# Streaming pooling trunk: operands of three products stored as split pairs by the first input phase and loaded as they are by the second

## Chip, cores and metric

One Trainium2 chip, one core of it. The metric is device time in microseconds, the median of the runs of one kernel. Engines: PE multiplies matrices (PEld is its weight load), DVE is VectorE, ACT ScalarE, POOL GpSimd; SP only issues transfers. Each engine works through its own instructions in order.

## What is computed

The depth is one layer, so only the pooling mixer runs, between two RMS norms. The sequence has 4096 frames of 1024 channels, everything in float32.

```
normed = rms_norm(x, norm_w)
u, gate = split(normed @ in_w, 2)              # in_w: 1024 x 2048
pooled  = trailing means of u (windows 2, 4, 8, 16 by channel group) - u
mixed   = pooled @ group_w + group_b           # per group, 256 x 256
y       = mixed * scale * silu(gate)
out     = rms_norm(x + y @ out_w, final_w)
```

## The kernel before

**Matrix products.** The large products are done in Winograd's form of Strassen's scheme: seven products (P1 to P7) of half-sized blocks in place of eight, with sums formed ahead. PE takes float32r operands, so a float32 operand is split into a high and a low part, and a product is made of high x high, high x low and low x high: three passes. The split is two instructions, an ACT copy that rounds (`copy(dst[:, 0], src)`) and a DVE subtraction that gives the rest (`sub(dst[:, 1], src, dst[:, 0])`), both on 128x1024 elements, in `split` (lines 203 to 206). Nearly all instructions are recorded under line 79, that of the wrapper `InOrder`, so the profile's groups are told apart by their tiles.

**Phases.** The group maps are first folded into the input weights (line 466 on PE). Then come three phases, listed step by step at lines 1450 to 1452: `("a", b, i)`, the first input phase, over four blocks `b` of 1024 frames and the seven products `i` in the order P1, P2, P7, P6, P5, P4, P3; `("b", b, i)`, the second input phase, over the same blocks with the other half of the input weights; and `("o", b, i)`, the output phase, over eight blocks of 512 frames. A plain product is 48 matmuls of 128x512 (line 814, in `mm3`).  In the second phase P7 of blocks 1 to 3 is itself done by seven smaller products (`split_seven`, `product_seven`, line 760). The first phase computes the operands of the seven products from x (loaded transposed, normalised and summed in `form_in`), splits them for its own products, and stores the unsplit float32 operand in DRAM (`sd`, 512 KB a half); the second loads it again and splits it again.

**Operand tiles.** The split operand of a half (`h` = 0, 1) is an `op` tile of 128 x 2048 float32r, 1024 KB: high part, then low part. There are four, taken in turn by `next_op` (line 561), so that a plain product uses two and the product after next uses the same two again. In a plain product PE reads the first half's tile for the first half of its time and the second half's for the rest; P1 goes by banks and reads both to the end. The seven-part P7 uses all four; two are filled for P6 while it runs, and `third` (line 701) sets the order anew, so that P5 gets the tile of parts P5 and P3 and the tile of parts P2 and P4.

**Other tiles.** Loads and results live in 11 `st` and 8 `vt` tiles, handed out and taken back by `take` and `give` (lines 178 to 189); a slot that is given back may be written again when its last reader is done, a DMA among them.

**What sets the order.** The loop at line 1903 goes through the steps. At each it calls `load` three steps ahead (`load_in`, line 602), `split_step` for the next step (`split_in`, line 645), `form` two steps ahead, then `run` (the product and the eviction of its banks). The program is then ordered engine by engine: the order of these calls is the priority, and an instruction that is ready may be placed before one that is not; `issue_after` keeps a pair in order. In the first phase `split_halves` (line 573) issues the stores `sd` on POOL's queue, whose instructions there also are the stores and loads of the reciprocal norms (`rd`). SP's queue carries the loads of x, of `sd` and of weights, and the stores of the pooled result `yd` and of transformed output weights (`wod`, `pair`). In block 2 of the first phase a weight sum, T3, is formed on DVE from loads of `wvd` (`load_t3`, `save_t3`, lines 340 and 345). The split weights of P5, P4 and P3 for the output phase are stored as pairs (`pairs_d`) and loaded on POOL's queue straight into weight tiles (`load_w`, line 402).

Of the kernel before, what the change touches and what calls it, by code (L numbers as in the profile page):

```python
# [10 lines left out]
F32 = mybir.dt.float32  # L11
# [4 lines left out]
P = 128  # L16
D = 1024
S = 4096
H = 512
TB = 1024  # L20
NB = S // TB
# [10 lines left out]
P1, P2, P3, P4, P5, P6, P7 = range(1, 8)  # L32
# [54 lines left out]
def kernel(  # L87
# [37 lines left out]
    vector, scalar, gpsimd, sync = (  # L125
        InOrder(tc, e) for e in (nc.vector, nc.scalar, nc.gpsimd, nc.sync)
    )
# [5 lines left out]
    dram = ctx.enter_context(tc.tile_pool(name="dram", bufs=1, space=bass.MemoryType.DRAM))  # L133
# [44 lines left out]
    def take(pattern="p (a b) -> p a b", pool=None, **sizes):  # L178
        sizes = sizes or {"a": 2}
        if pool is None:  # L180
            spare = len(vt.free) > keep[0] or not st.free
            pool = vt if spare and vt.age() < st.age() else st
        return pool.take(lambda t: t[:, 0:D].rearrange(pattern, **sizes))
# [4 lines left out]
    def give(ap):  # L188
        next(p for p in (st, vt, early, early5) if id(ap) in p.used).give(ap)

    def add(dst, a, b):
        vector.tensor_tensor(out=dst, in0=a, in1=b, op=ALU.add)

    def sub(dst, a, b):
        return vector.tensor_tensor(out=dst, in0=a, in1=b, op=ALU.subtract)
# [7 lines left out]
    def split(dst, src):  # L203

        latest_copy[0] = copy(dst[:, 0], src).ins
        latest_split[0] = sub(dst[:, 1], src, dst[:, 0].bitcast(F32)).ins
# [18 lines left out]
        for i in (P5, P4, P3)  # L225
    }
    sd = [
        {
            i: [dram.tile([P, 2, H], F32, name=f"sd{b}_{i}_{h}") for h in range(2)]
            for i in range(P1, P7 + 1)  # L230
            if (b, i) != (0, P6)
        }
        for b in range(NB)
    ]
# [180 lines left out]
    def woven(ap):  # L415

        return ap.rearrange("p (s a) -> p a s", s=2)
# [143 lines left out]
    def next_op(pattern, **sizes):  # L561
        t = ops.pop(0)
        ops.append(t)
        return t.rearrange(pattern, **sizes)
# [3 lines left out]
    def split_half(u):  # L568
        t = next_op("p (s a b) -> p s a b", s=2, a=2)
        split(t, u)  # L570
        return t

    def split_halves(us, saved=None):
        ts = []
        for h, u in enumerate(us):
            t = split_half(u)
            if saved is not None:
                first_saves.append(gpsimd.dma_start(out=saved[h], in_=u).ins)
            ts.append(t)
        return ts  # L580

    def load_x(b, half, kh, between=None):
        us = []
        for h in range(2):
            if h and between:
                between()
            u = take()
            k = 4 * kh + 2 * h
            sync.dma_start(out=u, in_=xt[2 * b + 1 - half, :, k : k + 2, :])
            us.append(u)  # L590
        return us

    def load_saved(b, i):
        us = []
        for h in range(2):
            u = take()
            sync.dma_start(out=u, in_=sd[b][i][h])
            us.append(u)
        return us
# [2 lines left out]

    def load_in(q, b, i):
        s = xs[b]
        if q and (b or i not in (P6, P4)):
            s[operand[i]] = load_saved(b, i)
        elif q:
            if i == P6:
                s["22"] = load_saved(b, P4)
        elif i in (P1, P2, P7, P6):  # L610
            key, *place = {
                P1: ("11", 0, 0), P2: ("12", 0, 1), P7: ("21", 1, 0), P6: ("22", 1, 1)
            }[i]
            s[key] = load_x(b, *place)
# [26 lines left out]
    def inner_in(q, b, i):  # L641

        return q == 1 and b > 0 and i == P7

    def split_in(q, b, i):
        s = xs[b]
        if inner_in(q, b, i):
            return split_seven(s)
        key = operand[i]
        later = q == 0 and b == 0 and i in (P1, P2)  # L650
        t = split_halves(s[key], None if q or later else sd[b].get(i))
        if later:
            stores.extend(zip(sd[0][i], s[key]))
        if i == P6 and q == 0 and b:
            form_s4(b)
        if q and (b or i != P7) or i not in (P1, P2, P7, P6):
            for u in s.pop(key):
                give(u)
        return t
# [5 lines left out]
    def split_seven(s):  # L665

        us = s["21"]
        a11, a21, a12, a22 = (
            us[h].rearrange("p k (s j a) -> p k s j a", s=2, j=2)[:, :, :, j]
            for h in range(2) for j in range(2)  # L670
        )
        front, back = (take("p (n k s a) -> p n k s a", n=2, k=2, s=2) for _ in range(2))
        sub(back[:, 0], a11, a21)
        sub(back[:, 1], a22, back[:, 0])
        add(front[:, 0], back[:, 1], a11)
        seven["mixed"] = sub(front[:, 1], a12, back[:, 1]).ins
        pattern = "p (s n k b a) -> p s n k b a"
        t = {}

        def sums(u, names):  # L680
            op = next_op(pattern, s=2, n=2, k=2, b=2)
            split(op.rearrange("p s n k b a -> p s (n k b a)"),
                  u.rearrange("p n k s a -> p (n k s a)"))
            give(u)
            for n, name in enumerate(names):
                t[name] = [[op[:, v, n, k].rearrange("p s a -> p a s") for k in range(2)]
                           for v in range(2)]

        def plain_op(h, names):
            op = split_half(us[h])  # L690
            for name, j in names.items():
                t[name] = [[woven(op[:, v, k])[:, j * P : (j + 1) * P] for k in range(2)]
                           for v in range(2)]

        sums(front, (P5, P3))
        plain_op(0, {P1: 0})

        def second():
            sums(back, (P7, P6))

        def third():
            plain_op(1, {P2: 0, P4: 1})
            for u in s.pop("21"):
                give(u)
            ops[:] = [ops[n] for n in (1, 2, 0, 3)]

        seven.update(second=second, third=third)
        return t
# [94 lines left out]
    def form_s4(b):  # L803
        for u, s2 in zip(xs[b]["12"], xs[b]["2"]):
            sub(u, u, s2)
# [652 lines left out]
    def load(n):  # L1458
        kind, b, i = step(n)
        if kind == "o":  # L1460
            load_o(b, i)
        elif kind:
            load_in(kind == "b", b, i)
# [13 lines left out]
    def split_step(n):  # L1477
        kind, b, i = step(n)
        if kind == "o":
            split_up[n] = split_o(b, i)  # L1480
        elif kind:
            with tc.issue_after(evicted[0]) if i == P6 else nullcontext():
                split_up[n] = split_in(kind == "b", b, i)
# [419 lines left out]
    for n in range(2, len(steps)):  # L1903
        kind, b, i = steps[n]
# [78 lines left out]
        if kind in ("a", "b"):  # L1983
# [11 lines left out]
            if kind == "b" and b == NB - 1 and i == P3:  # L1995
                f = take("p (a b) -> p a b", a=2)
                sync.dma_start(
                    out=f.rearrange("p a b -> p (a b)"), in_=final_w.partition_broadcast(P)
# [54 lines left out]
```

## Time and profile before

| | |
|---|---|
| median of 3 runs | 907.79 us (907.16 to 908.06) |
| span of the profiled execution | 905.6 us |
| time around the span, from that median | 2.2 us |
| busy PE, DVE, ACT, POOL | 99%, 81%, 57%, 17% of the span |
| moved by DMA | 209.60 MB, mean 231 GB/s |
| mean granted clock of PE | 0.999 |

The profile is of one execution; its own time apart from the span isn't listed, so the median stands for it. A group row reads: line, engine, operation, tile written <- tiles read, shape, count, then busy time in us, mean of one in ns, the engine's idle time just before, and what ended most of it. A row of the stages view reads: stretch, its length, busy time of each engine with its count, granted clock, share of the DMA engines' time, GB/s. A row of the timeline reads: start, duration, engine, line, operation, and in brackets the idle time before it and what ended it. "To landing" is the time from a DMA's issue to its last byte.

### The profile page before, as it was taken

What the parts mean: (1) busy time and instruction counts of PE and PEld (TensorE: products, weight loads), DVE (VectorE), ACT (ScalarE), POOL (GpSimd) and SP (SyncE); (2) the same over time, 40 slices, a digit from 0 to 9 for tenths busy, and PEclk for the clock granted to TensorE, in tenths of its full rate; (3) what the DMA queues carried; (4) which work ended last, traced back from release to release, by engine and by line L of the source; (5) the groups of instructions that cost most, each with busy time, mean ns of one, the idle gap of its engine ahead of it and who ended that gap; (6) DMA issues with size and microseconds to landing.
All of it is one profiled execution on the core that took longest, in us unless ns stands there. A gap on an engine that the chain in (4) does not pass through costs nothing.

```text
span 905.6 us, 12443 instructions
## 1 busy us (share of the span) xinstructions
PE 895.4 (99%) x4554; PEld 792.2 (87%) x4554; DVE 737.0 (81%) x910; ACT 519.2 (57%) x848; POOL 152.2 (17%) x250
## 2 busy tenths in 40 slices
PE   9999999999999999999999999999999999999996
PEld 7888888888888888889889888988889899998995
DVE  3899896984996996995485499698898788888798
ACT  7869547446445467446345654744557466565464
POOL 0030110110111000010100011021233343342330
PEclk9999999999999999999999999999999999999999
DMA  9989778678769475854245386699573855945953
GB/s 342 401 316 322 260 279 320 215 296 284 269 251 369 171 260 203 313 195 170 90 140 185 140 302 232 233 330 306 152 213 81 221 171 150 238 149 131 266 176 116
DMA packets 78620, 209.60 MB, mean 231 GB/s; under 512 B 7392, under 2 KB 25184, under 8 KB 77792
## 3 DMA queue, kind: packets, MB, share of 16 engines
q1 hardware_dynamic: 57872, 143.77, 45.7%
q0 software_dynamic: 19968, 63.98, 22.7%
q10 hardware_dynamic: 720, 1.06, 0.3%
q8 instruction: 35, 0.57, 0.3%
q14 instruction: 25, 0.20, 0.1%
HBM read 133.28 MB, written 75.51 MB: 231 GB/s over the span
## 4 chain that ended last, share of the span: by engine, by line
PE 88%; DVE 5%; DMA 3%; ACT 2%; issue 2%; POOL 0%; DVEq 0%; ACTq 0%; POOLq 0%; SPq 0%
PE bank L814 76%; PE bank L956 5%; PE bank L760 3%; PE bank L466 3%; DVE vt L79 2%; DVE op L79 2%; DVE st L79 1%; DMA vt<-yd 1%; DMA st<-wvd 1%; ACT vt L79 1%; DMA early<-in_group_w 0%; ACT st L79 0%; ACT op L79 0%; DMA out<-vt 0%; DVE columns L79 0%
## 5 line engine op out<-in xcount | busy, mean ns | idle before, releaser
L814 PE MATMUL bank<-op,w 128*128 128x512 f32 x2544 | 551.2, 379 | 1.5 <-ACT st L79 1.0
L814 PEld LDWEIGHTS bank<-op,w 128*128 128x128 f32 x2544 | 480.2, 189 | 70.9 <-ACT st L79 1.8
L814 PE MATMUL bank<-w,op 128*128 128x512 f32 (+1 forms) x1044 | 230.5, 377 | 0.0
L814 PEld LDWEIGHTS bank<-w,op 128*128 128x128 f32 x1044 | 192.3, 189 | 25.0
L79 DVE TENSOR_TENSOR op<-st,op 128x1024 fp32r<-128x1024 f32 x119 | 144.9, 1223 | 55.7 <-ACT op L79 55.4
L79 ACT ACTIVATE op<-st 128x1024 fp32r<-128x1024 f32 x119 | 124.8, 1052 | 81.6 <-PE bank L814 32.3
L79 ACT ACTIVATE op<-vt 128x1024 fp32r<-128x1024 f32 x66 | 69.4, 1053 | 70.0 <-DVE vt L79 41.7
L79 DVE TENSOR_TENSOR op<-vt,op 128x1024 fp32r<-128x1024 f32 x66 | 79.8, 1222 | 22.2 <-ACT op L79 22.1
L79 ACT ACTIVATE vt<-bank 128x512 f32<-128x512 f32 (+1 forms) x124 | 68.7, 577 | 46.0 <-PE bank L814 38.3
L79 DVE TENSOR_TENSOR st<-st,st 128x1024 f32<-128x1024 f32 (+2 forms) x49 | 54.8, 1134 | 30.4 <-ACT st L79 16.7
L79 ACT ACTIVATE bank<-bank 128x512 f32<-128x512 f32 (+1 forms) x84 | 41.1, 489 | 51.4 <-PE bank L814 38.6
L79 POOL COPY vt<-tails 128x32 f32<-128x32 f32 x14 | 17.5, 1257 | 271.7 <-DVE inner L79 106.8
L79 DVE TENSOR_TENSOR vt<-bank,vt 128x512 f32<-128x512 f32 (+1 forms) x92 | 52.9, 603 | 6.2 <-PE bank L956 4.6
L79 ACT ACTIVATE st<-bank 128x512 f32<-128x512 f32 (+1 forms) x60 | 34.2, 586 | 35.6 <-PE bank L814 25.0
L79 ACT ACTIVATE st<-st 128x1024 f32<-128x1024 f32 (+1 forms) x37 | 38.9, 1056 | 21.7 <-DVE st L79 19.7
L79 DVE TENSOR_TENSOR st<-bank,st 128x512 f32<-128x512 f32 (+1 forms) x70 | 42.6, 627 | 4.7 <-PE bank L956 2.5
L79 POOL DMA_DIRECT2D sd<-st x45 | 24.0, 533 | 125.7 <-DVE st L79 77.7
L956 PEld LDWEIGHTS bank<-w,op 128*128 128x128 f32 x312 | 40.4, 191 | 1.7
L956 PE MATMUL bank<-w,op 128*128 128x256 f32 x312 | 41.1, 275 | 0.0
L79 DVE TENSOR_TENSOR st<-st,vt 128x1024 f32<-128x1024 f32 (+1 forms) x33 | 38.5, 1187 | 2.8 <-DMA vt<-rd 2.8
L79 DVE TENSOR_TENSOR_SCAN vt<-vt,window 128x1040 f32<-128x1040 f32 x16 | 38.0, 2381 | 0.1
L79 DVE TENSOR_TENSOR vt<-vt 128x1024 f32<-128x1024 f32 (+3 forms) x42 | 37.7, 899 | 0.1
(119 smaller groups left out, 770.3 us busy)
## 6 DMA issues: line engine op xcount, KB each, us to landing
sd<-st POOLq DMA_DIRECT2D x45, 512.0 KB, 4.7
st<-sd SPq DMA_DIRECT2D x43, 512.0 KB, 4.7
st<-in_xt SPq DMA_DIRECT2D x28, 512.0 KB, 7.6
st<-in_x SPq DMA_DIRECT2D x21, 512.0 KB, 7.7
yd<-st SPq DMA_DIRECT2D x19, 512.0 KB, 3.0
vt<-yd SPq DMA_DIRECT2D x17, 512.0 KB, 10.7
out<-vt POOLq DMA_DIRECT2D x16, 512.0 KB, 3.3
st<-yd SPq DMA_DIRECT2D x15, 512.0 KB, 8.0
```

The costliest lines, as they stand in the source:

```text
L79: r = f(*args, **kwargs)
L466: latest[0] = nc.tensor.matmul(ps, a[:, kk, 2 * j + t, :], maps, start=t + m == 0, stop=t == 1 and m == len(pairs) - 1,).ins
L760: latest[0] = nc.tensor.matmul(cell(n, c).rearrange("p (a s) -> p a s", s=2), x1, x2, start=i == P1 and k + m == 0, stop=k == 1 and m == 2 ...
L814: latest[0] = nc.tensor.matmul(ps, a, b, start=start and n == 0, stop=stop and n == 2, skip_group_check=True).ins
L956: latest[0] = nc.tensor.matmul(ps, x1, x2, start=start and k + n == 0, stop=k == 1 and n == 2, skip_group_check=True,).ins
```

## The change

For blocks 1 to 3 and the products P5, P4 and P3, the first phase stores the split pair (the `op` tile, 1024 KB a half) in a new DRAM tile `pd` in place of the unsplit operand in `sd`, still on POOL's queue. In the second phase `load_in` loads nothing for these products, and `split_in` takes two `op` tiles and loads the pairs straight into them on SP's queue, with no copy and no subtraction. Block 0, the other products and the output phase keep their code. The numbers that PE multiplies are the same.

```
+            if (b, i) != (0, P6) and not (b and i in (P5, P4, P3))
...
+    paired = (P5, P4, P3)
+    pd = [
+        {
+            i: [dram.tile([P, 2, 2, H], F32, name=f"pd{b}_{i}_{h}") for h in range(2)]
+            for i in paired if b
         }
         for b in range(NB)
     ]
...
-    def split_halves(us, saved=None):
+    def split_halves(us, saved=None, pairs=None):
         ts = []
         for h, u in enumerate(us):
             t = split_half(u)
-            if saved is not None:
+            if pairs is not None:
+                gpsimd.dma_start(out=pairs[h], in_=t.bitcast(F32))
+            elif saved is not None:
                 first_saves.append(gpsimd.dma_start(out=saved[h], in_=u).ins)
             ts.append(t)
         return ts
...
     def load_in(q, b, i):
         s = xs[b]
+        if q and i in pd[b]:
+            return
...
         if inner_in(q, b, i):
             return split_seven(s)
+        if q and i in pd[b]:
+            t = [next_op("p (s a b) -> p s a b", s=2, a=2) for _ in range(2)]
+            for h in range(2):
+                sync.dma_start(out=t[h].bitcast(F32), in_=pd[b][i][h])
+            return t
         key = operand[i]
         later = q == 0 and b == 0 and i in (P1, P2)
-        t = split_halves(s[key], None if q or later else sd[b].get(i))
+        t = split_halves(s[key], None if q or later else sd[b].get(i),
+                         None if q else pd[b].get(i))
```

More of the change, by code (lines that the diff above doesn't have):

```diff
@@ L230 @@
             for i in range(P1, P7 + 1)
-            if (b, i) != (0, P6)
+            if (b, i) != (0, P6) and not (b and i in (P5, P4, P3))
+        }
+        for b in range(NB)
+    ]
+    paired = (P5, P4, P3)
[3 more added lines that the diff above has]
+            for i in paired if b
         }
```

## Prediction

> **What bounds the kernel now.** I read the busy shares first, then the waits of PE alone, then the busy time by stage.
>
> ```profile
> PE 895.4 (99%) x4554; PEld 792.2 (87%) x4554; DVE 737.0 (81%) x910; ACT 519.2 (57%) x848; POOL 152.2 (17%) x250
> ```
> ```profile
> PE bank L814 <- ACT st L79: 1.0, 2, 0.6
> ...
> PE bank L814 <- DVE op L79: 0.5, 1, 0.5
> ```
> ```profile
> 0.00:5.00 5.00, 3.85 (x9) 1.33 (x10) 0.12 (x2) 1.49 (x2) 0.20 (x4) 1.00 0.58 191
> ...
> 32.40:105.80 73.40, 73.40 (x345) 64.11 (x344) 65.03 (x84) 56.22 (x86) 13.22 (x25) 1.00 0.87 320
> 105.80:178.30 72.50, 72.50 (x338) 63.48 (x337) 63.00 (x75) 40.23 (x66) 9.68 (x18) 1.00 0.78 270
> 178.30:251.00 72.70, 72.27 (x336) 62.96 (x335) 55.15 (x67) 37.59 (x60) 8.75 (x17) 1.00 0.77 282
> 251.00:324.00 73.00, 73.00 (x340) 63.93 (x339) 63.59 (x69) 39.23 (x60) 6.26 (x12) 1.00 0.70 254
> 324.00:398.40 74.40, 73.34 (x339) 63.60 (x338) 65.80 (x75) 43.80 (x60) 2.77 (x2) 1.00 0.74 261
> 398.40:470.20 71.80, 71.80 (x374) 63.99 (x373) 48.31 (x55) 33.17 (x50) 3.64 (x4) 1.00 0.43 147
> 470.20:542.00 71.80, 71.80 (x373) 63.99 (x373) 49.77 (x50) 40.22 (x61) 4.85 (x4) 1.00 0.55 198
> 542.00:613.70 71.70, 71.70 (x373) 63.87 (x372) 60.72 (x65) 41.03 (x58) 8.99 (x9) 1.00 0.75 259
> 613.70:890.00 276.30, 276.27 (x1543) 249.03 (x1542) 236.35 (x316) 154.23 (x286) 93.07 (x155) 1.00 0.66 183
> 890.00:905.60 15.60, 8.03 (x49) 7.18 (x47) 11.09 (x40) 9.17 (x26) 0.00 (x0) 0.92 0.44 167
> ```
>
> The columns of the last view are the stretch, its length, the busy time of PE, PEld, DVE, ACT and POOL, the granted clock, the DMA share and GB/s. The stretches are the blocks of the first input phase (32.4 to about 324), block 0 of the second (to 398.4), its blocks 1, 2 and 3 (to 613.7), and the output phase. PE's idle time is 1.15 us at the start, 0.43 in block 2 of the first phase, 1.06 in block 0 of the second, 0.03 in the output phase and 7.57 at the end; these make the 10.2 us between 895.4 and 905.6. In blocks 1 to 3 of the second phase, where the change takes work away, it is 0.00. Two rows of the chain of waits give PE's own pace there:
>
> ```profile
> 428.76 62.16 PE bank L814 x288
> ...
> 500.52 62.16 PE bank L814 x288
> ```
>
> That is 62.16/288 = 0.2158 us a matmul and 48 x 0.2158 = 10.36 us a product, and the block comes round every 500.52 - 428.76 = 71.76 us. Nothing is waited for.
>
> A busy PE could still be a slow PE. The Trainium skill says so ("Trainium Kernel Development and Optimization", Performance Expectations): matmul busy time is a poor metric because matmuls are pipelined, and weight-load busy time is a better one. By that rule the 11% that PEld leaves in block 1 (63.99 of 71.80) would be slack, up to 7.8 us a block. The trace speaks against it here: blocks 1 and 3 need 71.8 and 71.7 us although DVE is busy 48.3 us in one and 60.7 in the other, so the pace does not move with DVE's load. I price this as a rival below.
>
> **What is taken away.** Three products (P5, P4, P3) in three blocks, two halves each: 18 splits, each an ACT copy and a DVE subtraction.
>
> ```profile
> L79 DVE TENSOR_TENSOR op<-st,op 128x1024 fp32r<-128x1024 f32 x119 | 144.9, 1223 | 55.7 <-ACT op L79 55.4
> L79 ACT ACTIVATE op<-st 128x1024 fp32r<-128x1024 f32 x119 | 124.8, 1052 | 81.6 <-PE bank L814 32.3
> ```
>
> DVE loses 18 x 1.223 = 22.0 us and ACT 18 x 1.052 = 18.9 us, all of it in blocks 1 to 3. PE is idle 0.00 us there, so on the path this is worth 0. Two slots of the shared st and vt tiles are also no longer taken per product; their loads had up to three steps (31 us) of lead, so that too is worth 0. In the first phase the slot of a half comes free after its split instead of after its store: also 0, but it may help the 0.43 us of block 2.
>
> **What is added: bytes.** 18 stores and 18 loads grow from 512 KB to 1024 KB: 18 x 0.524 = 9.4 MB more written and 9.4 MB more read, on 209.6 MB. The issues stay 18 on POOL and 18 on SP.
>
> ```profile
> sd<-st POOLq DMA_DIRECT2D x45, 512.0 KB, 4.7
> st<-sd SPq DMA_DIRECT2D x43, 512.0 KB, 4.7
> ...
> w<-pair POOLq DMA_DIRECT2D x6, 1024.0 KB, 8.0
> ```
> ```profile
> DMA to landing us min/median/max: 5.0/8.0/8.7
> ```
>
> The six weight loads w<-pair are the nearest row to the new loads and stores: the same 1024 KB of split pairs, into a tile that PE has just left. They land in 8.0 us, 5.0 to 8.7 (last row, the same tile's answer).
>
> **What is added: waits in the second phase.** A load may be issued only when PE has left the op tile, and SP stands still until then. When that is can be read from the copies that fill the same tiles now:
>
> ```profile
> 427.45 1.07 ACT L79 ACTIVATE op<-vt 128x1024 fp32r<-128x1024 f32 x1
> ...
> 430.33 1.08 ACT L79 ACTIVATE op<-st 128x1024 fp32r<-128x1024 f32 x1
> 433.98 1.06 ACT L79 ACTIVATE op<-st 128x1024 fp32r<-128x1024 f32 x1 [2.57 <-PE bank L814]
> ```
>
> These are, in block 1, the two halves of P5 and the first of P4. The P7 before them is the seven-part product, which holds all four op tiles: P5's first tile is left with its sixth part, at about 427.4, the second with its end at 428.76. P6 then runs 10.36 us, so P5 begins at 439.12 and reads its second half at 444.3. The budgets are 11.7 and 15.5 us. P4 and P3 have half a product and a whole one: 15.5 us for each half. Against 8.7 us at worst that leaves 3.0 us in the tightest place, three times. Between issue and these starts the DMAs are not full except in block 3:
>
> ```profile
> 427.30:439.00 11.70, 11.70 (x63) 10.41 (x62) 5.54 (x6) 6.90 (x11) 0.00 (x0) 1.00 0.50 170
> 499.00:510.80 11.80, 11.80 (x63) 10.51 (x62) 5.60 (x6) 6.95 (x11) 0.00 (x0) 1.00 0.37 129
> 571.00:582.60 11.60, 11.60 (x62) 10.31 (x60) 7.75 (x8) 8.73 (x13) 0.00 (x0) 1.00 0.90 307
> ```
>
> The w<-pair loads ran right behind the third of these, in a stretch of the same kind, and their 8.7 holds for it. I take 0. Queued behind the waiting load on SP are later operand loads (31 us of lead), the pool stores yd and, in block 2, the weight stores; PE waits for none of them. From both sides: below nothing is excluded by the 0.00; above, see the first rival.
>
> **What is added: waits in the first phase.** The store now waits for the split and reads the op tile, and the copy that fills the tile two products later must wait for the store. Block 2 is the tightest.
>
> ```profile
> 194.60 0.53 POOL L79 DMA_DIRECT2D sd<-st  x1 [6.95 <-issue]
> ...
> 209.75 0.53 POOL L79 DMA_DIRECT2D sd<-st  x1 [0.60 <-DVE st L79]
> ```
> ```profile
> 221.09 1.22 DVE L79 TENSOR_TENSOR op<-st,op 128x1024 fp32r<-128x1024 f32 x1
> ```
> ```profile
> 232.40 1.04 ACT L79 ACTIVATE op<-st 128x1024 fp32r<-128x1024 f32 x1
> ```
>
> Six of the saves in 194.60 to 209.75 are those of P5, P4 and P3; they leave as soon as the sums are formed. They will leave after the splits, from about 211 to 237. P5's second half is split by 222.3; its store lands by 222.3 + 8.7 = 231.0, and the copy of P3's second half into that tile starts at 232.40. A later landing first uses up 1.4 us, and then the lead of that split: P3 begins at about 241.9, reads its second half at 247.1, and the split took 4.4 us from 232.40. (The seven-part product takes 71.76 - 62.16 = 9.60 us, so block 1 of the second phase begins at 428.76 - 9.60 - 2 x 10.36 = 398.4, the first phase ends 7 x 10.36 + 1.06 before that, at 324.8, and P3 of block 2 begins eight products earlier.) So PE feels nothing until the landing is about 20 us. On POOL the rstd stores and loads stand behind these stores; the normalising that waits for them has a like lead. Cost 0.
>
> The bytes need room as well:
>
> ```profile
> 210.60:240.00 29.40, 28.97 (x135) 25.05 (x134) 15.93 (x25) 17.75 (x31) 1.93 (x4) 1.00 0.81 291
> 240.00:251.00 11.00, 11.00 (x53) 9.63 (x52) 11.00 (x16) 4.28 (x5) 1.49 (x4) 1.00 0.52 190
> ```
> ```profile
> 136.00:142.00 6.00, 6.00 (x30) 1.00 1.02 414
> ```
>
> Six stores are 6.3 MB in 29.4 us, 214 GB/s on top of 291: 505, where the highest stretch shown is 414. The estimate is a backlog of 29.4 x 0.091 = 2.7 MB or 6.5 us, and the following 11 us at 190 GB/s have room for 2.5 MB of it. 6.5 us lies inside the lead of about 10. The Trainium skill ("DMA: Bandwidth & Descriptors", Where 436 GB/s comes from) has about 358 GB/s as the limit of transfers to and from HBM; by it the backlog would be an estimated 12 us, some 2 us over the lead. The trace's 414 is above that limit, and the measurement decides.
>
> **Sum.** 905.6 - 0 (work removed) + 0 (loads in time) + 0 (stores in time) = 905.6 us of span. The median of the runs shown is 907.79, 2.2 us more for what lies around the span; the forecast is **907.8 us**.
>
> **Rivals.**
> *PE waits for P5 after the seven-part product (slower).* Place: the start of P5 in blocks 1, 2 and 3. It decides from the point where SP's delay and the landing together pass 11.7 us. For it: two 1024 KB loads leave within 1.4 us of each other, while the w<-pair loads were some 5 us apart; SP is in order and a store that waits for DVE can hold the load; and single loads into st have been late:
>
> ```profile
> 588.35 0.54 POOL L79 DMA_DIRECT2D w<-pair  x1 [27.01 <-PE bank L814]
> ...
> 593.54 0.55 POOL L79 DMA_DIRECT2D w<-pair  x1 [0.47 <-PE bank L814]
> ```
> ```profile
> DMA to landing us min/median/max: 2.0/5.1/15.2
> ```
>
> At 15.2, the longest landing of st tiles, a block loses 3.5 us and three lose 10.5: 918. At half of that, 913. Against it: the DMA shares 0.50 and 0.37 of two of the three gaps.
>
> *The first phase's traffic makes a load late (slower).* The place is known:
>
> ```profile
> 219.94 1.23 DVE L79 TENSOR_TENSOR st<-st,st 128x1024 f32<-128x1024 f32 x1 [9.38 <-DMA st<-wvd]
> ```
>
> DVE stood 9.38 us before this sum, and PE lost the 0.43 us of block 2 through it; every further us would cost PE one. A 1 MB store of P5 falls beside it, but two of 0.5 MB fall there now. One to four us: 909 to 912.
>
> *All gaps in the middle close (within the bound).* 0.43 + 1.06 = 1.49 us, 906.3. Block 0's operands are not changed, so 1.06 has no reason to go.
>
> *PE's pace rises with less DVE and ACT work (faster).* By the weight-load row up to 7.8 us in each of three blocks, 884; against it stand the equal blocks 1 and 3.
>
> *The change does not do what it says.* The new branch returns before the split, so the 18 splits must go; I give this next to nothing.
>
> **Chances.** What a measurement of this kernel can tell from no change is about 0.2%, 1.8 us: 906.0 to 909.6. Forecast with closing gaps 0.56; late P5 loads 0.24; first-phase traffic, or a new order of the queues that holds PE, 0.14; faster by more than 1.8 us 0.06, since only the 1.49 us, the 7.57 at the end or the pace could give it. So faster 0.06, same 0.56, slower 0.38. The likeliest case's own range is 906.2 to 909.3. The wider range goes from 906.0 to 914, past the half price of the first rival.
>
> **What the new profile would show.** Right: PE busy for the whole of its blocks 1 to 3, about 71.8 us each; 18 fewer copies and subtractions into op; DVE some 22 us less busy; loads of 1024 KB landing in 8 to 9 us; the first phase no longer than now. Wrong: PE rows that wait for a DMA into op at the start of P5; ACT copies in the first phase that wait for a store; a longer wait for wvd; blocks shorter than 71.7 us, which would refute the bound itself.

## The result and the profile after

The changed kernel takes **920.58 us** (median of 4 runs, 917.26 to 920.99) against 907.53 before (4 runs): ratio 1.0133, 95% interval 1.0116 to 1.0150. It is slower by 13 us, where no change was forecast. Its profiled execution took 920.99 us with a span of 919.2, 13.6 us more than the span before.

The page's busy shares, then the waits of PE (engine, tile and line waited for: us in total, times, longest us):

```profile
PE 900.8 (98%) x4554; PEld 794.8 (86%) x4554; DVE 718.1 (78%) x892; ACT 501.2 (55%) x830; POOL 147.7 (16%) x250
```
```profile
PE bank L832 <- DVE op L79: 4.6, 2, 4.1
PE bank L832 <- ACT bank L79: 3.7, 1, 3.7
PE bank L832 <- ACT st L79: 1.1, 2, 0.5
```

The work removed is there: 18 instructions fewer on DVE and 18 fewer on ACT, 18.9 and 18.0 us less busy (22.0 and 18.9 were forecast). But PE now waits 3.7 and 4.1 us in two places, neither of which is in the blocks where the change loads anything. The same stretches as before the change, by stage (columns as in the prediction):

```profile
178.30:251.00 72.70, 72.04 (x333) 62.45 (x332) 52.39 (x63) 37.60 (x64) 8.78 (x17) 1.00 0.84 297
251.00:324.00 73.00, 69.31 (x314) 59.98 (x313) 58.44 (x61) 35.08 (x54) 6.95 (x13) 0.98 0.84 293
324.00:398.40 74.40, 69.23 (x307) 59.30 (x306) 62.57 (x70) 41.91 (x57) 0.00 (x0) 0.95 0.72 262
398.40:470.20 71.80, 71.80 (x374) 63.99 (x373) 46.16 (x52) 28.77 (x48) 6.22 (x5) 1.00 0.55 197
470.20:542.00 71.80, 71.80 (x374) 63.98 (x373) 42.07 (x47) 35.42 (x55) 0.63 (x3) 1.00 0.56 209
542.00:613.70 71.70, 71.70 (x373) 63.92 (x372) 54.87 (x57) 35.24 (x52) 6.36 (x9) 1.00 0.80 299
```

From 398.4 to 613.7 there is no idle time, as before. The loss lies in block 3 of the first phase and in block 0 of the second, the second and third rows (block 2 loses little); there the third column from the right, PE's granted clock, is 0.98 and 0.95 too. Finer windows of PE alone (stretch, length, PE busy with matmul count, clock, DMA share, GB/s) show both waits and what follows them:

```profile
264.00:266.00 2.00, 0.27 (x2) 1.00 1.01 392
266.00:268.00 2.00, 0.04 (x1) 1.00 0.70 271
268.00:270.00 2.00, 2.00 (x6) 0.64 0.97 374
270.00:272.00 2.00, 2.00 (x6) 0.51 0.35 135
272.00:274.00 2.00, 2.00 (x11) 1.00 0.90 284
...
331.00:333.00 2.00, 0.00 (x0) 1.00 0.00 0
333.00:335.00 2.00, 0.00 (x0) 0.60 0.62 248
335.00:337.00 2.00, 1.89 (x5) 0.50 1.00 344
337.00:339.00 2.00, 2.00 (x6) 0.50 0.88 233
339.00:341.00 2.00, 2.00 (x8) 0.69 0.82 241
341.00:343.00 2.00, 2.00 (x11) 1.00 1.03 419
```

After each wait PE is "busy" but does 6 matmuls in 2 us in place of 11: the clock is at half for some 3.4 us from 268.6 on, and for some 6.8 us from 333.4 on, in the second wait already. The sum closes. Block 1 of the second phase goes on after its P7 at 441.94 us where it was 428.59, 13.35 later. Of that 0.82 us is there already at the old short wait in block 2 (PE goes on at 223.86, before at 223.04), 3.69 + 4.11 = 7.80 is new waiting, and the remaining 4.73 is the longer busy time of the same 667 matmuls between there and the next old wait (148.96 us in place of 144.23). Most of it, some 4.3 us, is the slow clock: it was 0.62 on average from 267.96 to 272.5 and 0.53 from 335.11 to 340.5.

**Where the first wait comes from.** POOL's timeline in the changed kernel, then in the kernel before. `rd<-rs` stores the reciprocal norms of the next block, `vt<-rd` loads them back spread over the partitions.

```profile
224.47 0.55 POOL L79 DMA_DIRECT2D rd<-rs  x1 [0.42 <-DVE rs L79]
225.61 0.54 POOL L79 DMA_DIRECT2D pd<-op  x1 [0.59 <-DVE op L79]
235.33 0.56 POOL L79 DMA_DIRECT2D vt<-rd  x1 [9.18 <-DMA rd<-rs]
```
```profile
223.66 0.54 POOL L79 DMA_DIRECT2D rd<-rs  x1 [13.38 <-DVE rs L79]
...
229.19 0.56 POOL L79 DMA_DIRECT2D vt<-rd  x1 [4.99 <-DMA rd<-rs]
```

The load, which waits for the store of a few numbers, can go 10.9 us after it in place of 5.5; then it takes another 7.0 us, 6.3 before. In the kernel before it landed at 235.5, 1.4 us before DVE came to it. Now it lands at 242.3, and DVE, which works in order, stands still for its normalising:

```profile
242.35 1.23 DVE L79 TENSOR_TENSOR st<-st,vt 128x1024 f32<-128x1024 f32 x1 [4.54 <-DMA vt<-rd]
```

It began at 236.90 before; DVE is 5.45 us late from here. The delay is passed on by a pooled result, `yd`, whose store leaves SP at 260.72 (255.26 before) and takes 6.45 us; an ACT copy that reuses its tile waits, and behind that copy, in order, is the one that PE needs:

```profile
260.72 6.45 DMA yd<-vt
```
```profile
267.20 0.23 ACT L79 ACTIVATE vt<-tails 128x32 f32<-128x32 f32 x1 [4.55 <-DMA yd<-vt]
267.33 1.06 ACT L79 ACTIVATE bank<-bank 128x512 f32<-128x512 f32 x2
...
267.96 4.33 PE L832 MATMUL bank<-op,w 128*128 128x512 f32 x11 [3.69 <-ACT bank L79]
```

**Where the second comes from.** DVE doesn't catch up in block 3. It forms the weight sums there and waits for a load of T3 (`t3d`), 6.11 us where it was 1.61; the two rows are from the changed kernel and from the one before:

```profile
307.31 1.42 DVE L79 SCALAR_TENSOR_TENSOR st<-st,colt,st 128x512 f32<-128x512 f32 x2 [6.11 <-DMA st<-t3d]
```
```profile
296.61 1.42 DVE L79 SCALAR_TENSOR_TENSOR st<-st,colt,st 128x512 f32<-128x512 f32 x2 [1.61 <-DMA st<-t3d]
```

It is 10.7 us late by then. That load was issued at 296.96, between two pair stores at 295.03 and 297.34, and took 10.3 us to land. A load of `wvd` costs DVE another 1.39 us at 325.38, where it cost none before. The subtraction that the second phase's first product needs starts at 333.84 in place of 321.64, and PE waits for it from 331.0 to 335.11.

### The profile page after: what moved, and what is told of

Same layout as the page of the kernel before. It is cut to its first block, busy times and chain, and to the rows that moved or that the text cites. A ratio compares the mean times of both kernels' runs of the same rounds, so it can differ in the third digit from the quotient of the medians.

```text
span 919.2 us, 12382 instructions
## 1 busy us (share of the span) xinstructions
PE 900.8 (98%) x4554; PEld 794.8 (86%) x4554; DVE 718.1 (78%) x892; ACT 501.2 (55%) x830; POOL 147.7 (16%) x250
## 4 chain that ended last, share of the span: by engine, by line
PE 70%; DVE 12%; DMA 7%; issue 6%; ACT 3%; POOL 1%; SPq 0%; DVEq 0%; POOLq 0%; ACTq 0%
PE bank L832 61%; DVE vt L79 5%; PE bank L974 4%; DVE st L79 3%; PE bank L778 3%; DVE op L79 3%; DMA vt<-yd 1%; DMA st<-yd 1%; PE bank L474 1%; DVE w L79 1%; DMA st<-wvd 1%; ACT st L79 1%; DMA early<-in_wut 1%; ACT vt L79 1%; DMA vt<-rd 1%
## 5 line engine op out<-in xcount | busy, mean ns | idle before, releaser
L79 DVE TENSOR_TENSOR op<-st,op 128x1024 fp32r<-128x1024 f32 x105 | 127.8, 1221 | 51.2 <-ACT op L79 50.8
L79 ACT ACTIVATE op<-st 128x1024 fp32r<-128x1024 f32 x105 | 109.9, 1051 | 77.9 <-PE bank L832 23.5
L79 ACT ACTIVATE op<-vt 128x1024 fp32r<-128x1024 f32 x62 | 65.2, 1054 | 75.2 <-DVE vt L79 46.3
L79 DVE TENSOR_TENSOR op<-vt,op 128x1024 fp32r<-128x1024 f32 x62 | 74.8, 1220 | 16.3 <-ACT op L79 16.1
L79 DVE TENSOR_TENSOR st<-st,st 128x1024 f32<-128x1024 f32 (+2 forms) x44 | 49.2, 1135 | 19.9 <-DMA st<-wvd 11.5
L79 POOL COPY vt<-tails 128x32 f32<-128x32 f32 x14 | 11.6, 835 | 240.9 <-DVE inner L79 79.7
L79 DVE TENSOR_TENSOR st<-st,vt 128x1024 f32<-128x1024 f32 (+2 forms) x35 | 40.9, 1189 | 11.1 <-DMA vt<-rd 9.7
L974 PE MATMUL bank<-inner,op 128*128 128x256 f32 x234 | 31.9, 276 | 0.0
## 6 DMA issues: line engine op xcount, KB each, us to landing
pd<-op POOLq DMA_DIRECT2D x18, 1024.0 KB, 10.2
st<-in_xt SPq DMA_DIRECT2D x28, 512.0 KB, 10.3
vt<-yd SPq DMA_DIRECT2D x17, 512.0 KB, 10.5
```

Of the source, the lines that this page charges most:

```text
L79: r = f(*args, **kwargs)
L974: latest[0] = nc.tensor.matmul(ps, x1, x2, start=start and k + n == 0, stop=k == 1 and n == 2, skip_group_check=True,).ins
```

## The experiments

The theory after this reading: the pair stores of the first phase make short, in-order transfers late, and nothing in the second phase costs anything. Rivals: the direct loads or the changed use of tiles cost it; it is POOL's queue, not the bytes; it is the store's later moment and its waits, not the bytes. Each comparison is with runs of the kernel before on the same chip.

| run | median us | ratio to before (95%) |
|---|---|---|
| stores alone | 919.74 | 1.0121 (1.0082 to 1.0161) |
| loads alone, two stores added | 909.69 | 1.0022 (1.0010 to 1.0034) |
| loads alone, no store added | 907.92 | 1.0004 (0.9995 to 1.0014) |
| norms on SP's queue | 920.15 | 1.0133 (1.0104 to 1.0161) |
| pair stores on ACT's queue | 918.48 | 1.0118 (1.0092 to 1.0143) |
| old kernel, bytes doubled, early | 923.46 | 1.0180 (1.0158 to 1.0202) |
| stores late, high part alone | 908.05 | 1.0008 (0.9999 to 1.0018) |
| change in block 1 alone | 910.03 | 1.0025 (1.0015 to 1.0034) |
| change in block 2 alone | 908.96 | 1.0022 (1.0009 to 1.0036) |
| change in block 3 alone | 913.29 | 1.0058 (1.0043 to 1.0073) |
| change in blocks 2 and 3 | 916.82 | 1.0102 (1.0085 to 1.0119) |
| change, other bytes given back | 915.97 | 1.0091 (1.0076 to 1.0106) |

### Which half

Stores alone. To the changed kernel:

```diff
     def load_saved(b, i):
-            sync.dma_start(out=u, in_=sd[b][i][h])
+            src = pd[b][i][h][:, 0] if i in pd[b] else sd[b][i][h]
+            sync.dma_start(out=u, in_=src)
     def load_in(q, b, i):
-        if q and i in pd[b]:
-            return
     def split_in(q, b, i):
-        if q and i in pd[b]:
-            t = [next_op("p (s a b) -> p s a b", s=2, a=2) for _ in range(2)]
-            ...
-            return t
```

> First half of the change alone: the first phase stores the pairs as the changed kernel does; the second phase loads only the high part (512 KB) and splits it again as the kernel before does (the low part is left out of these operands). Theory (the cost comes from the pair stores in the first phase): about 920 us, with PE idle some 3.7 us near 265 us and some 4 us near 332 us. Rival (the cost comes from the direct loads into the op tiles, or from the changed use of the st and vt tiles): about 907.5 us, no PE wait over 0.6 us.

Measured 919.74 us; in its profile, of an execution of 917.26, PE waits 4.7 us for DVE's op at the start of the second phase and 1.9 us for ACT's bank near 264. The theory holds: the first half of the change carries the cost.

Loads alone. To the changed kernel:

```diff
-            if (b, i) != (0, P6) and not (b and i in (P5, P4, P3))
+            if (b, i) != (0, P6)
...
-            elif saved is not None:
+            if saved is not None:
...
-                sync.dma_start(out=t[h].bitcast(F32), in_=pd[b][i][h])
+                sync.dma_start(out=t[h].bitcast(F32), in_=pd[1][P5][h])
...
-                         None if q else pd[b].get(i))
+                         pd[1][P5] if not q and (b, i) == (1, P5) else None)
```

> Second half alone: the first phase stores unsplit operands as the kernel before does, plus one pair (block 1, P5); all 18 direct loads of the second phase read that one pair, so the operands of the other eight products are not theirs. Theory (pair stores): 907 to 908.5 us, PE without a wait in blocks 1 to 3 of the second phase. Rival (direct loads): about 920 us.

Measured 909.69: between the two, 2 us over the kernel before. Its trace has PE waiting 1.5 us in block 2 of the first phase and nothing in blocks 1 to 3 of the second, so the two added stores in block 1 were suspected, and the run was made anew without them. The pairs are then read from a weight pair that is in DRAM anyhow:

```diff
+                sync.dma_start(out=t[h].bitcast(F32), in_=pairs_d[P5][0])
```

> The direct loads alone, with no store added: the first phase is as before (512 KB, early), and all 18 direct loads read one split weight pair that lies in DRAM already, so the operands of the nine products are not theirs. Theory (loads cost nothing; the 2 us of the earlier run of the loads alone came from its two added stores in block 1): 907 to 908 us and no PE wait in blocks 1 to 3 of the second phase. Rival (the loads cost the 2 us): 909 to 910.

Measured 907.92, ratio 1.0004: no difference. PE's waits are those of before:

```profile
PE bank L830 <- ACT st L79: 1.0, 2, 0.6
...
PE bank L830 <- DVE op L79: 0.5, 1, 0.5
```

So the loads, their new use of tiles and the 18 splits taken away come to nothing together, which is the prediction's bound put to the test; PE's waits show no cost on one side that a gain on the other could hide.

### Queue or bytes

The reciprocal norms moved off POOL's queue, to the changed kernel:

```diff
     def store_rs(b, half, rs):
-        gpsimd.dma_start(out=rd[b][half][0].rearrange("(p j) -> p j", j=4), in_=rs)
+        sync.dma_start(out=rd[b][half][0].rearrange("(p j) -> p j", j=4), in_=rs)
     def load_rstd(b, half):
-        gpsimd.dma_start(out=rstd[b][:, half], in_=rd[b][half][0].partition_broadcast(P))
+        sync.dma_start(out=rstd[b][:, half], in_=rd[b][half][0].partition_broadcast(P))
```

> The changed kernel, with the stores and loads of the reciprocal norms (rd) issued on SP's queue in place of POOL's. Theory (in POOL's queue the small rd store lands only behind the 1024 KB pair stores issued ahead of it, and the normalising of the next block waits): the rd landings fall from 3.3/6.5/10.5 us to about 2 to 5, the 3.7 us PE wait near 265 goes, 911 to 915 us. Rival (all DMAs are late because the 16 engines are full, whichever queue): the rd landings stay above 6 us in the median and the time stays at 917 to 922.

Measured 920.15. Here my theory fell: the landings of rd, in the changed kernel and in this run,

```profile
DMA to landing us min/median/max: 3.3/6.5/10.5
```
```profile
DMA to landing us min/median/max: 3.4/6.3/12.2
```

are nearly the same. PE's waits lie otherwise, 2.10 us near 255 and 0.92 near 268 in place of 3.69, and 5.51 at the start of the second phase, but the time is the same. The other way round, the pair stores on ACT's queue:

```diff
             if pairs is not None:
-                gpsimd.dma_start(out=pairs[h], in_=t.bitcast(F32))
+                scalar.dma_start(out=pairs[h], in_=t.bitcast(F32))
```

> The changed kernel, with the pair stores issued on ACT's queue in place of POOL's. Theory (POOL's queue is the place): the rd landings fall to about 4 us and the 3.7 us PE wait near 265 goes, 909 to 915 us, unless ACT, which then waits for DVE's subtraction at each of 18 stores, holds an eviction. Rival (the bytes are the place): 917 to 922.

Measured 918.48, rd landing in 2.8/7.2/11.1 us. So it isn't the queue: the `rd` transfers are late on either queue while the pair stores are under way.

### Bytes or moment

The kernel before, with a second, early copy of the same operands:

```diff
+    sd2 = [
+        {i: [dram.tile([P, 2, H], F32, name=f"se{b}_{i}_{h}") for h in range(2)]
+         for i in (P5, P4, P3) if b}
+        for b in range(NB)
+    ]
...
+            if again is not None:
+                gpsimd.dma_start(out=again[h], in_=u)
```

> The kernel before, with the unsplit operands of P5, P4, P3 of blocks 1 to 3 stored twice (the second copy is never read): the changed kernel's bytes in the first phase, but leaving as early as before and with no wait for the split. Theory (bytes: in blocks 2 and 3 the 16 DMA engines have no room for 3 MB more a block, whatever the queue): 912 to 920 us, with PE waits over 1 us in blocks 2, 3 or at the start of the second phase. Rival (timing: the stores leave after the splits, into the stretch where the next block's x is loaded): about 908 us.

Measured 923.46, more than the 912 to 920 expected and than the change itself, with no pair, no wait of a store for a split and the code of the second phase as it was. PE waits 3.14 and 2.68 us in block 2 and 3.42 us at the start of the second phase. In block 2 DVE now stands 15.5 us for the load of `wvd`:

```profile
DVE st L79 <- DMA st<-wvd: 18.7, 2, 15.5
```

The second copy is also an instruction more on POOL's queue and holds its `st` tile longer; what these two cost was not separated from the bytes. The reverse, the changed kernel's moment with the old bytes. To the kernel of the first experiment:

```diff
-            i: [dram.tile([P, 2, 2, H], F32, name=f"pd{b}_{i}_{h}") for h in range(2)]
+            i: [dram.tile([P, 2, H], F32, name=f"pd{b}_{i}_{h}") for h in range(2)]
...
-                gpsimd.dma_start(out=pairs[h], in_=t.bitcast(F32))
+                gpsimd.dma_start(out=pairs[h], in_=t[:, 0].bitcast(F32))
...
-            src = pd[b][i][h][:, 0] if i in pd[b] else sd[b][i][h]
+            src = pd[b][i][h] if i in pd[b] else sd[b][i][h]
```

> The changed kernel's first phase with its timing (the store waits for the split and reads the op tile) but only the high part, 512 KB, stored; the second phase loads that and splits it again (the low part is left out of these operands). Bytes as before, timing as after. Theory (bytes): 907 to 909 us. Rival (timing): 912 to 920 us. If both matter: between, about 910 to 913.

Measured 908.05, ratio 1.0008. This is the closest pair of runs: the op tile is read late and must be read before it is filled again in both, and only the size of the store differs (the high part is also ready one DVE instruction sooner). 1024 KB costs 12 us, 512 KB nothing that the interval shows. The trace shows the chain back at its old timing: in block 2 the `rd` store lands in 5.2 us and the load goes 5.65 us after it, DVE doesn't wait for the norms, and its wait for T3 is 2.33 us. So neither the later moment nor the new waits cost it; a store of twice the bytes does, by itself or by the op tile that it holds longer. In the changed kernel ACT waits for such a store only once, 1.35 us at 234.66.

The whole change with as many bytes given back elsewhere in the first phase:

```diff
-        t = split_halves(s[key], None if q or later else sd[b].get(i),
+        t = split_halves(s[key], None if q or later or b and i in (P1, P2, P6) else sd[b].get(i),
...
-            sync.dma_start(out=u, in_=sd[b][i][h])
+            sync.dma_start(out=u, in_=(sd[0][P7 if i == P6 else i] if b and i in (P1, P2, P6) else sd[b][i])[h])
```

> The changed kernel, but the first phase does not store the operands of P1, P2 and P6 of blocks 1 to 3 (the second phase loads block 0's in their place, so those operands are not theirs): 3.1 MB a block less, as much as the pairs add. Theory (room for bytes, and nothing about pairs, waits or queues): 907 to 909 us. Rival (the store's wait for the split, the wait of the next split for the store): 912 to 920.

Measured 915.97: a miss. By its total this run moves what the kernel before moves in the first phase, and still loses 8 us. The windows say why: first the changed kernel, then this run (PE alone, columns as above).

```profile
185.00:205.00 20.00, 19.89 (x92) 1.00 0.72 269
205.00:225.00 20.00, 19.45 (x90) 1.00 0.72 246
225.00:245.00 20.00, 20.00 (x94) 1.00 1.00 348
245.00:265.00 20.00, 19.27 (x90) 1.00 0.97 364
265.00:285.00 20.00, 17.04 (x71) 0.91 0.73 255
285.00:305.00 20.00, 20.00 (x95) 1.00 0.95 323
305.00:325.00 20.00, 20.00 (x94) 1.00 0.77 278
```
```profile
185.00:205.00 20.00, 20.00 (x94) 1.00 0.43 160
205.00:225.00 20.00, 20.00 (x95) 1.00 0.78 255
225.00:245.00 20.00, 20.00 (x94) 1.00 1.01 381
245.00:265.00 20.00, 19.33 (x90) 1.00 0.69 259
265.00:285.00 20.00, 20.00 (x94) 1.00 0.57 189
285.00:305.00 20.00, 20.00 (x94) 1.00 0.87 335
305.00:325.00 20.00, 20.00 (x95) 1.00 0.83 307
```

The bytes went away between 185 and 205 and between 245 and 285. The stretch of block 2's pair stores, 225 to 245, is as full as ever (1.01; 0.74 before the change), and so, in shorter windows, is that of block 3's from 290 to 300 (1.00 and 1.01). The trace shows where the loss sits now. DVE still waits 3.90 us for the norms, but with 245 to 265 at 0.69 in place of 0.97 PE waits only 0.67 us near 264. In block 3 DVE waits 9.70 us for a weight load (`in_in_w`) that was issued among the pair stores, 3.11 before, and PE waits 6.20 us at the start of the second phase. So what counts is the bytes in the stretch, not in the phase. Whether the emptier stretch behind 245 is what shortened the first wait wasn't tested by itself.

### Which block

To the changed kernel, with 1, 2 or 3 in place of the 1, and `b > 1` for blocks 2 and 3:

```diff
-            if (b, i) != (0, P6) and not (b and i in (P5, P4, P3))
+            if (b, i) != (0, P6) and not (b == 1 and i in (P5, P4, P3))
...
-            for i in paired if b
+            for i in paired if b == 1
```

> The whole change, but for block 1 only (stores and loads of pairs; blocks 2 and 3 as before). In the changed kernel PE waits at the end of what follows block 2's and block 3's stores, and not behind block 1's. Theory: block 1 costs 0 to 2 us, 907.5 to 909.5. Rival (each block costs the same third of 13): about 912.

> The whole change, but for block 2 only. Theory: block 2's stores, beside the T3 loads and the eight loads of block 3's x, cost the PE wait of 3.7 us and some 2.6 us of half clock behind it: 912 to 915 us. Rival (equal thirds): about 912 as well, but with e7 at 912 too; if the cost comes only when the delays of two blocks add up: 908.

> The whole change, but for block 3 only. Blocks 1 and 2 alone cost 2 us each. Theory (delays of the blocks add up on DVE, and each block alone stays mostly inside its lead): 908 to 911 us. Rival (block 3 is the dear one, as PE waits 4.1 us at the start of the second phase): 914 to 918.

> The whole change, but for blocks 2 and 3. Theory (DVE comes out of block 2 some 6 us late and has no stretch in which to catch up before block 3's traffic): 914 to 919 us, more than blocks 2 and 3 alone cost together. Rival (the blocks are independent): the sum of the two, about 910.

Measured 1.0025, 1.0022 and 1.0058 for one block, 1.0102 for blocks 2 and 3. Block 1 costs some 2 us, a little over the 907.5 to 909.5 expected. PE's wait for it, 1.96 us, comes in block 2 beside the T3 loads, but the delay is older. Of DVE's waits in this run,

```profile
DVE st L79 <- DMA st<-wvd: 12.9, 2, 9.2
DVE st L79 <- DMA vt<-rd: 2.3, 1, 2.3
```

the one for `wvd` is no longer than before the change (9.38), while that for the norms is new: it ends at 164.59, behind block 1's own pair stores, where the `rd` store took 10.0 us to land, and DVE goes on 3.03 us later than before. It is the chain of block 2 again.

Block 2 alone costs far less than I expected. In its profile, of an execution of 908.10, DVE waits 4.42 us for the norms, as in the whole change, and PE only 1.13; its executions go from 907.59 to 913.34. Block 3 is the dear one with 0.58% by itself, 913.29, between the theory's 908 to 911 and the rival's 914 to 918. The three singles add to 1.05%, the whole is 1.33%, and 2 and 3 together 1.02% against 0.80% for the sum. The intervals allow a surplus for delays that add up, and also none; so my "more than together" is not shown.

In block 3 alone PE's one long wait is the one at the start of the second phase, 3.60 us, with the same forerunner on DVE:

```profile
328.51 44.39 PE L832 MATMUL bank<-op,w 128*128 128x512 f32 x198 [3.60 <-DVE op L79]
```
```profile
DVE st L79 <- DMA st<-t3d: 5.5, 1, 5.5
```

No run points to a version that beats the kernel before: blocks 1 to 3 of its second phase have no idle time that removed work could take away, and the added bytes of the first phase cost time in every run that had them.

## Why the prediction failed, point by point

*What bounds the kernel.* Right. The pace of blocks 1 to 3 is unchanged at 71.8 us, the removed work was worth 0 there, and the loads alone change nothing (1.0004). The weight-load rival is refuted: DVE's busy time fell to 42.1 us in block 2, and PE needs the same 71.80.

*Direct loads, cost 0.* Right. They land in 6.3 us in the median against the 8.0 taken, and PE waits for none. The longest took 11.9 us, over the 8.7 taken as the worst, but it was one of P3 in block 3, which had 15.5; those of P5 took at most 8.4, where the tightest had 11.7. The first rival, late P5 loads, which had most of the chance of "slower", did not happen.

*Stores of the first phase, cost 0.* **This is the step that failed**: "6.5 us lies inside the lead of about 10", and with it "the normalising that waits for them has a like lead". Wrong was the lead held against the backlog. I took the lead of one split before its product, about 10 us, and gave it to everything. The load of the norms had 1.4 us: before the change it landed at 235.5 for a sum that began at 236.90. Now it landed 6.8 us later, most of that by the small store in front of it, which landed in 10.5 us in place of 5.1 (the load in 7.0 in place of 6.3). Take off the 1.4 and the 0.9 us by which DVE was late already, and the 4.54 us that DVE waited are left. DVE works in order, so that delays all that stands behind it, and it had not recovered when block 3's traffic cost it 4.5 us more at T3.

The sizes were off as well. The stores left about when I said, from 212.0 to 238.1, but landed in 10.2 us in the median against 8.0 (8.7 at worst), and the backlog lasted longer: the stretch 225 to 245 is full (1.00) and the next, 245 to 265, nearly so (0.97), where I had it gone soon after 251. Of the signs named for being wrong, an ACT copy that waits for a store came once, 1.35 us, and PE did not wait for it.

*The traffic rival.* Its mechanism was the right one, a load made late by traffic and DVE held by it, but its place was not. I named the T3 loads of `wvd` in block 2. There DVE waits 9.13 us in the changed kernel and 9.24 with the change in block 1 alone, where it was 9.38; only the doubled early bytes made it longer, 15.5. The norms and block 3's weight sums, which cost the 3.69 and 4.11, I had not followed. It was priced at 1 to 4 us; the two waits alone make 7.8.

*The clock.* It was in no term of the sum. Of the 13 us, 4.73 are longer busy time of the same matmuls behind the two waits, some 4.3 of it by the half clock.

## What to carry to other kernels

An engine at 99% hides what others save and shows what others lose, so before trading arithmetic for bytes in such a kernel, look at the stage that gains (has its bound any idle time?) and at each stage that pays. For the paying stage don't compare bytes with an average: go through the stretch where the new bytes travel, list the loads that an in-order engine waits for, follow a chain of two transfers from its first store, and hold the backlog against that load's own lead (here 1.4 us, not 10). And in this kernel a wait of PE of over about 2 us cost more than its length.

## What was not expected of the hardware

**How long a wait halves the clock.** In the waits looked at, those up to 1.96 us left the granted clock at 1.00; from 2.10 us on it fell to about half for some 3 to 7 us. The first row is the stretch after the 1.96 us wait (change in block 1 alone), the second that after a wait of 2.10 us (norms on SP's queue):

```profile
225.60:228.00 2.40, 2.32 (x11) 1.00 0.94 212
```
```profile
255.00:258.00 3.00, 2.95 (x7) 0.52 0.66 236
```

The Trainium skill ("TensorE: Matmul & The Clock Gate", Part 1: The HAM clock gate) describes the halved clock, puts it after one idle window of about 3.4 us, and says that the window runs freely. The halving agrees with these traces; the length does not: 2.10 us was enough here. With a free-running window there need be no fixed limit, and these few waits don't fix one.

**A few numbers wait like a megabyte.** While the pair stores were under way, 10.9 us went by from the issue of a 2 KB store to the load that waits for it (5.5 before). At the same place it was 12.1 us with that store on SP's queue, and 8.0 with the pair stores on ACT's queue: neither brought it back. With stores of half the size it was 5.65.
